# Hybrid mLSTM and delta-rule block on one core: outputs fetched back during the last group, the first z job split ahead, last quarters in token order, sigmoids by tanh

## The chip, the core and the metric

The kernel runs on one core of one Trainium2 chip. The metric is device time in microseconds (us). The kernel before takes 2027.0 us, the median of three runs (2022.27 to 2036.63). Engines are called as in the profile: PE is TensorE, PEld its weight loads, DVE is VectorE, ACT is ScalarE, POOL is GpSimd and SP is SyncE. SP issues the loads of weights, POOL and ACT issue the other transfers.

## What is computed

One layer, batch 1, 256 tokens, width 2048, in fp32. Cut to what matters here:

```python
h = rms_norm(x, norm_mix_w) * (1 + scale_m) + shift_m     # mod = silu(c) @ W_ada + b_ada gives shift, scale, gate
proj = h @ w_in
# branch A: mLSTM, 4 heads, both directions
h_a = rms_norm(mlstm_fwd(q_a, k_a, v_a, i, f) + mlstm_bwd(...))
y_a = (sigmoid(a_o) * h_a) @ w_branch_a
# branch B: gated delta rule, 16 heads, both directions
qkv = silu(depthwise_conv(b_qkv))                          # q and k are l2-normalised
log_decay = -exp(A_log) * softplus(b_a + dt_bias)
o_b = rms_norm(gdn_fwd(q_b, k_b, v_b, beta, log_decay) + gdn_bwd(...))
y_b = (o_b * silu(b_z)) @ w_branch_b
# merge, output projection, SwiGLU, final norm
x = x + gate_m * ((sigmoid(merge_a) * y_a + sigmoid(merge_b) * y_b) @ w_out)
x = x + gate_f * ((silu(hf @ w_gate) * (hf @ w_up)) @ w_down)    # hf = modulated rms_norm(x)
return rms_norm(x, norm_final_w)
```

## The kernel before

**The tiling.** Every large product is a sum of three: a weight tile `raw` of 1 MB comes by SP's queue, ACT rounds half of it to `wh` (L157, L182), DVE forms the remainder `wl = raw - wh` (L158, L183), and PE multiplies both with the high and low part of the activations. A *half* (two of the four k blocks of a `raw` tile, both tokens' tiles of 128) is 12 matmuls: four with `wh` and the high part (L200), four with `wh` and the low part (L201), four with `wl` and the high part (L203). `raw`, `wh` and `wl` have three buffers each, and the sums over the modulation weights (`ada`, L125 and L126, 1 MB each) use the same three `raw` buffers. A job (`tjob`, or `fjob` for output in transposed form) goes through eight halves and ends with a function `done` that takes the result out of PSUM. Names of tiles carry the job: z for the gate of the delta rule, v, o and a for the mLSTM's values, output gate and q/k, ma and mb for the merge gates, b for the delta rule's q, k and v, then yb, ya, o, gt, up and d.

**The order.** Jobs stand in the list `fills`, and `fill(n)` emits n of their halves between the small matmuls of the recurrences. A scheduler then sets the order of the instructions on each engine from the whole program. Only what is wrapped in `order(...)` stays in the order in which it was written. Each engine runs its own list in order, and so does each queue of DMAs: an instruction that waits holds up what stands behind it.

**The stages**, by the profiled execution: the first projections (up to 131 us), the first z job with the gates, softplus and the convolutions (131 to 180), the delta rule in four groups of four heads (180 to 985), the mLSTM with the projection y_b (985 to 1140), y_a, the output projection o (its last quarter at 1290 to 1298), gate and up, and d, whose last quarter and the final norm end the kernel.

**The first z job.** `z_job(0, 3)` makes three halves ahead (`early`), and these and all its later halves are pinned by `order`. Each later half is made only when its own step is reached. Meanwhile `gates` works out softplus by a polynomial on DVE (L377 to L395), the decay `alpha` by ACT's Exp (L397), stores it by POOL (L398) and reads it back broadcast (`al`, L279). The first reader is the scan `dec` on DVE (L544). The convolutions run on ACT and DVE (L298, L300, L301).

**The delta rule's outputs.** Each head's output `obt` is stored to DRAM by ACT (`ob_d[g]`, L773), 128 KB a head. After the fourth group, the pools of the delta rule are closed. Then `o_load` (L891 to L893) fetches each group's four heads back, 512 KB, by POOL's queue into `o4` (two buffers in the pool `ml`), and `o_split` (L897, L898) makes the high part `obh` on ACT and the low part `obl` on DVE. `obh` and `obl` are the activations of y_b, group 0 being the first four k blocks. The pool `fr` (padded rows, convolution results, q, k, v and decays of the delta rule) lives until the end of the fourth group.

**The mLSTM** loads q/k, v, the output gate (`sgo`, L906) and decays by POOL, two heads at a time. `sgo` has two buffers, so the load for heads 2 and 3 waits until heads 0 and 1 have used theirs (L971). `psc`, `pden` and `ph` are its matmuls.

**Activations.** `keep` (L308) takes the results of the v, o, ma and mb jobs through ACT (L313) and stores them. For o, ma and mb the function is Sigmoid. Silu is used by the convolutions (L301) and the z jobs (L328), Exp by the gates, Sqrt by the norms. A change of function between these sets puts an ACT_TABLE_LOAD in front of the instruction.

**Last quarters.** The jobs o and d end with a quarter that is taken token by token (`by_token`, L216 to L226): all 12 matmuls of token 0 are written before those of token 1, without `order`. When a token is done, `residual` (L1084 to L1086) and the norm follow on DVE and ACT.

## Time and profile before

| what | value |
|---|---|
| median of 3 runs | 2027.0 us |
| profiled execution, its own time | 2026.32 us |
| its span | 2024.5 us |
| PE busy | 1948.6 us (96%) |
| DVE busy | 1386.4 us (68%) |
| ACT busy | 1036.8 us (51%) |
| POOL busy | 95.2 us (5%) |
| mean granted PE clock | 0.985 |
| DMA | 485.65 MB, mean 240 GB/s |

The span is the profiled execution from its first to its last instruction, and its own time is 1.8 us longer. A busy share says how long an engine worked, not that it worked at its full clock: the granted clock is listed apart. Idle time of an engine matters only where a later end depends on it. For PE, the waits after the first 131 us, listed by what they waited for, are the shortest way in.

### The profile page before, as it was taken

The numbers are of one execution on the slowest core, as the hardware profiler recorded it, in microseconds if no ns is written. First come the engines' busy times: TensorE is split into PE (matmuls) and PEld (weight loads), VectorE is DVE, ScalarE is ACT, GpSimd is POOL, SyncE is SP. The second block draws the span as 40 slices with busy tenths as digits, with TensorE's granted clock in tenths as the row PEclk, the third lists the DMA queues.
The fourth block names the chain that finished last, engine by engine and source line by source line (L and its number), as shares of the span: only waits on it lengthen the run. The fifth ranks groups of instructions, "written<-read, shape, count | busy, mean of one in ns | idle before, by whom it ended". The sixth has DMA issues, their size and how long they took to land.

```text
span 2024.5 us, 27066 instructions
## 1 busy us (share of the span) xinstructions
PE 1948.6 (96%) x10374; PEld 1709.0 (84%) x10374; DVE 1386.4 (68%) x2059; ACT 1036.8 (51%) x1571; POOL 95.2 (5%) x181
## 2 busy tenths in 40 slices
PE   8998999999999999999799999899999999999997
PEld 6777889989889988989678888788888888888886
DVE  5777887778878778865577679766666665555554
ACT  3146748755774667555443444454444444444443
POOL 0001201100100011000200000000000000000000
PEclk9999999999999999999899999999999999999999
DMA  9986674567666665776887679556767666555653
GB/s 400 420 338 193 194 238 158 172 189 260 203 218 214 220 219 206 242 275 214 300 294 265 226 261 419 203 208 240 259 239 259 248 229 229 191 206 206 208 203 130
DMA packets 78324, 485.65 MB, mean 240 GB/s; under 512 B 10201, under 2 KB 15585, under 8 KB 23793
## 3 DMA queue, kind: packets, MB, share of 16 engines
q1 hardware_dynamic: 63360, 450.95, 61.2%
q0 software_dynamic: 7520, 17.88, 4.0%
q10 hardware_dynamic: 7314, 15.10, 2.0%
q8 instruction: 81, 1.33, 0.3%
q14 instruction: 49, 0.40, 0.1%
HBM read 467.07 MB, written 16.82 MB: 239 GB/s over the span
## 4 chain that ended last, share of the span: by engine, by line
PE 72%; DVE 11%; DMA 9%; ACT 5%; issue 3%; POOL 0%; SPq 0%; ACTq 0%; DVEq 0%; POOLq 0%
PE acc_up L201 4%; PE acc_up L203 4%; PE acc_up L200 4%; PE acc_d L200 4%; PE acc_d L201 4%; PE acc_d L203 4%; PE acc_gt L200 4%; PE acc_gt L201 4%; PE acc_gt L203 4%; DMA ra<-ada 3%; PE acc_a L161 2%; PE acc_o L203 2%; PE acc_o L200 2%; PE acc_o L201 2%; PE acc_b L161 2%
## 5 line engine op out<-in xcount | busy, mean ns | idle before, releaser
L126 DVE SCALAR_TENSOR_TENSOR ada<-ada,crow 128x2048 f32<-128x2048 f32 x64 | 146.5, 2289 | 50.6 <-DMA ada<-ada 50.6
L183 DVE TENSOR_TENSOR wl_d<-raw_d,wh_d 128x1024 fp32r<-128x1024 f32 x88 | 107.7, 1224 | 102.3 <-ACT wh_d L182 100.3
L183 DVE TENSOR_TENSOR wl_up<-raw_up,wh_up 128x1024 fp32r<-128x1024 f32 x88 | 107.6, 1225 | 99.3 <-ACT wh_up L182 99.3
L182 ACT ACTIVATE wh_d<-raw_d 128x1024 fp32r<-128x1024 f32 x88 | 92.9, 1056 | 128.5 <-PE acc_d L201 122.9
L182 ACT ACTIVATE wh_gt<-raw_gt 128x1024 fp32r<-128x1024 f32 x88 | 92.9, 1056 | 120.7 <-PE acc_gt L201 73.2
L182 ACT ACTIVATE wh_up<-raw_up 128x1024 fp32r<-128x1024 f32 x88 | 93.0, 1056 | 119.2 <-PE acc_up L201 72.5
L183 DVE TENSOR_TENSOR wl_gt<-raw_gt,wh_gt 128x1024 fp32r<-128x1024 f32 x88 | 107.0, 1224 | 67.5 <-ACT wh_gt L182 46.7
L161 PE MATMUL acc_b<-hh,wh_b 128*128 128x256 f32 x576 | 140.0, 285 | 5.5 <-ACT wh_b L157 5.5
L161 PE MATMUL acc_b<-hl,wh_b 128*128 128x256 f32 x576 | 137.6, 281 | 0.0
L200 PE MATMUL acc_gt<-wh_gt,hfh 128*128 128x512 f32 x352 | 136.0, 386 | 0.0
L201 PE MATMUL acc_gt<-wh_gt,hfl 128*128 128x512 f32 x352 | 135.2, 384 | 0.0
L200 PE MATMUL acc_up<-wh_up,hfh 128*128 128x512 f32 x352 | 133.4, 379 | 0.0
L201 PE MATMUL acc_up<-wh_up,hfl 128*128 128x512 f32 x352 | 133.4, 379 | 0.0
L200 PE MATMUL acc_d<-wh_d,ffh 128*128 128x512 f32 x344 | 130.8, 380 | 0.0
L201 PE MATMUL acc_d<-wh_d,ffl 128*128 128x512 f32 x344 | 130.8, 380 | 0.0
L511 PE MATMUL first<-x,raw 128*128 128x256 f32 x512 | 114.5, 382 | 7.1 <-ACT x L504 7.1
L161 PEld LDWEIGHTS acc_b<-hh,wh_b 128*128 128x128 f32 x576 | 111.7, 194 | 8.5 <-ACT wh_b L157 6.6
L158 DVE TENSOR_TENSOR wl_b<-raw_b,wh_b 128x1024 fp32r<-128x1024 f32 x72 | 87.3, 1219 | 45.5 <-ACT wh_b L157 45.4
L511 PEld LDWEIGHTS first<-x,raw 128*128 128x128 f32 x512 | 96.0, 190 | 25.6 <-ACT x L504 13.1
L161 PEld LDWEIGHTS acc_b<-hl,wh_b 128*128 128x128 f32 x576 | 111.7, 194 | 1.8 <-issue 1.7
L157 ACT ACTIVATE wh_b<-raw_b 128x1024 fp32r<-128x1024 f32 x72 | 75.3, 1056 | 55.8 <-DMA raw_b<-winb 29.3
L182 ACT ACTIVATE wh_o<-raw_o 128x1024 fp32r<-128x1024 f32 x64 | 67.4, 1057 | 66.1 <-PE acc_o L201 30.7
(369 smaller groups left out, 5025.7 us busy)
## 6 DMA issues: line engine op xcount, KB each, us to landing
ada<-ada SPq DMA_DIRECT2D x64, 1024.0 KB, 5.2
raw_gt<-wgu SPq DMA_DIRECT2D x44, 1024.0 KB, 5.0
raw_up<-wgu SPq DMA_DIRECT2D x44, 1024.0 KB, 5.0
raw_d<-wd SPq DMA_DIRECT2D x44, 1024.0 KB, 4.9
raw_b<-winb SPq DMA_DIRECT2D x36, 1024.0 KB, 5.2
ra<-ada SPq DMA_DIRECT2D x32, 1025.0 KB, 15.7
raw<-win SPq DMA_DIRECT2D x16, 1024.0 KB, 14.5
raw_z<-wint SPq DMA_DIRECT2D x16, 1024.0 KB, 5.7
```

The costliest lines, as they stand in the source:

```text
L126: V.scalar_tensor_tensor(raw, raw, 1.0, row_c[:, :D], ALU.mult, ALU.mult, accum_out=mod[:, c0 + b : c0 + b + 1])
L157: S.activation(wh, raw[:, k0 : k0 + 8], AF.Copy)
L158: V.tensor_tensor(wl, raw[:, k0 : k0 + 8], wh.bitcast(F32), ALU.subtract)
L161: PE.matmul(o, wh[:, k], both(x, k0 + k).rearrange("p a b -> p b a"), start=k0 + k + i == 0, stop=False)
L182: order(S.activation(wh, raws[u][:, k0 : k0 + 2], AF.Copy), early)
L183: order(V.tensor_tensor(wl, raws[u][:, k0 : k0 + 2], wh.bitcast(F32), ALU.subtract), early)
L200: order(PE.matmul(ps[t], tok(xh, kk, t), turns(wh[:, k]), start=kk == 0, stop=False), early and steps > 1)
L201: PE.matmul(ps[t], tok(xl, kk, t), turns(wh[:, k]), start=False, stop=False)
L203: PE.matmul(ps[t], tok(xh, kk, t), turns(wl[:, k]), start=False, stop=kk == last)
L511: PE.matmul(first[o], raw[:, o], x[:, b], start=b == 0 and o % 2 == 0, stop=b == KB - 1 and o % 2 == 1)
```

## The change

It has four parts.

1. A z job with `early` and one step keeps two further halves made ahead at each step, all of them pinned. Only `z_job(0, 3)` is such a job.
2. The matmuls of the last quarters (`by_token`) are pinned: all of token 0, then all of token 1.
3. `fr` gets an exit stack of its own and is closed when the fourth group (g == 3) begins. In its room a pool `op` of three buffers takes `o4` of groups 0 to 2. Their loads are issued in the fourth group, and that of group 3 goes into one buffer of `ml` after it. The three splits are made in front of the mLSTM, two halves apart. `sqh` goes from two buffers to one.
4. Sigmoid becomes tanh of half the argument. `keep` scales by 0.5, and the `+1` goes into the multiplication with the projections y_b and y_a (L1003 and L1013 of the changed kernel), the factor 0.5 into the row `gm`, through which the output projection passes anyway. The mLSTM's gate gets an instruction of its own on ACT (L980 of the changed kernel, 128x1024, one per head).

The diff, cut to its core:

```diff
             if k0:
                 pump()
                 if u == len(chunks) - 1:
                     done(ps)
+            while early and steps == 1 and len(made) < min(2, len(todo) - 1 - n):
+                made.append(halves(*todo[n + 1 + len(made)]))
             yield True
...
-                    PE.matmul(ps[t], tok(xh, kk, t), wh, start=False, stop=False)
-                    PE.matmul(ps[t], tok(xl, kk, t), wh, start=False, stop=False)
+                    order(PE.matmul(ps[t], tok(xh, kk, t), wh, start=False, stop=False))
+                    order(PE.matmul(ps[t], tok(xl, kk, t), wh, start=False, stop=False))
                 for k in range(4):
                     kk = last - 3 + k
-                    PE.matmul(ps[t], tok(xh, kk, t), turns(w[k // 2][1][:, k % 2]), start=False, stop=kk == last)
+                    order(PE.matmul(ps[t], tok(xh, kk, t), turns(w[k // 2][1][:, k % 2]), start=False, stop=kk == last))
...
-    fr = pool(sx, "fr", side="right")
+    sf, so = ExitStack(), ExitStack()
+    fr = pool(sf, "fr", side="right")
...
     def keep(dst, fn, name):
+        scale = 0.5 if fn == AF.Tanh else 1.0
...
-                S.activation(ev[:, t], ps[t], fn)
+                S.activation(ev[:, t], ps[t], fn, scale=scale)
...
-            keep((v_d, o_d)[i][h], (AF.Copy, AF.Sigmoid)[i], f"{'vo'[i]}{h}"),
+            keep((v_d, o_d)[i][h], (AF.Copy, AF.Tanh)[i], f"{'vo'[i]}{h}"),
...
-            keep((ma_d, mb_d)[i][g], AF.Sigmoid, f"m{'ab'[i]}{g}"),
+            keep((ma_d, mb_d)[i][g], AF.Tanh, f"m{'ab'[i]}{g}"),
...
+    def o_load(g, where, bufs):
+        o4 = where.tile([P, 4, T], F32, tag="o4", bufs=bufs, name=f"o4_{g}")
+        G.dma_start(o4, ob_d[g].rearrange("h p t -> p h t"))
+        return o4
+
+    o4s = []
     invert(0)
     for g in range(4):
+        if g == 3:
+            sf.close()
+            op = pool(so, "op", side="right")
...
             pieces = stream(4 * g + 2 * p + 4)
+            if g == 3:
+                o4s += [o_load(i, op, 3) for i in ((0, 1), (2,))[p]]
...
-        sq = ml.tile([P, DV_A], F32, tag="sqh", bufs=2, name=f"sqh{h}")
+        sq = ml.tile([P, DV_A], F32, tag="sqh", bufs=1, name=f"sqh{h}")
...
         V.reciprocal(ss, ss)
+        S.activation(so, so, AF.Copy, scale=0.5, bias=0.5)
...
-                V.tensor_tensor(mg[:, t, g * 512 : (g + 1) * 512], gt[:, t], ps[t], ALU.mult)
+                V.scalar_tensor_tensor(mg[:, t, g * 512 : (g + 1) * 512], gt[:, t], 1.0, ps[t], ALU.add, ALU.mult)
...
-                V.tensor_tensor(gt[:, t], gt[:, t], ps[t], ALU.mult)
+                V.scalar_tensor_tensor(gt[:, t], gt[:, t], 1.0, ps[t], ALU.add, ALU.mult)
...
     cores = steps(mlstm(0), mlstm(1))
-    o4s = [o_load(g) for g in range(2)]
     every[0] = 0
-    fill(2)
+    o4s.append(o_load(3, ml, 1))
     next(cores)
-    fill(6)
-    for g in range(2):
+    for g in range(3):
+        fill(2)
         o_split(g, o4s[g])
-        o4s.append(o_load(g + 2))
-        fill(1)
+    fill(4)
     next(cores)
-    fill(5)
-    o_split(2, o4s[2])
     fill(1000)
+    so.close()
...
-                V.tensor_scalar(dg[:, e], ident, mod[:, c : c + 1], None, ALU.mult)
+                V.tensor_scalar(dg[:, e], ident, mod[:, c : c + 1], factor, ALU.mult, ALU.mult)
...
-    row(2, gm, wp)
+    row(2, gm, wp, 0.5)
```

**Where instructions move.** First DVE, in the first z job. `u`, `s` and `poly` are steps of the softplus polynomial, `cv` the convolutions, and `wl_z_2_0` the remainder that z's fifth half (third tile, first half) needs. Before:

```order
L386 SCALAR_TENSOR_TENSOR poly<-poly,s_801 128x256 x2
L300 SCALAR_TENSOR_TENSOR cv_2_1070<-pad_136,pk,cv_2_1070 128x256
L386 SCALAR_TENSOR_TENSOR poly<-poly,s_801 128x256
L300 SCALAR_TENSOR_TENSOR cv_2_1070<-pad_136,pk,cv_2_1070 128x256
L300 SCALAR_TENSOR_TENSOR cv_0_1339<-pad_138,pk,cv_0_1339 128x256
L386 SCALAR_TENSOR_TENSOR poly<-poly,s_801 128x256
L183 TENSOR_TENSOR wl_z_2_0_812<-raw_z_2_809,wh_z_2_0_811 128x1024
L183 TENSOR_TENSOR wl_z_2_2_828<-raw_z_2_809,wh_z_2_2_827 128x1024
L183 TENSOR_TENSOR wl_z_3_0_854<-raw_z_3_851,wh_z_3_0_853 128x1024
```

In the changed kernel:

```order
L381 TENSOR_TENSOR u<-u,gden 128x256
L183 TENSOR_TENSOR wl_z_2_0_784<-raw_z_2_781,wh_z_2_0_783 128x1024
L183 TENSOR_TENSOR wl_z_2_2_808<-raw_z_2_781,wh_z_2_2_807 128x1024
L303 SCALAR_TENSOR_TENSOR cv_0_987<-pad_140,pk,cv_0_987 128x256
L303 SCALAR_TENSOR_TENSOR cv_1_1020<-pad_134,pk,cv_1_1020 128x256
L386 TENSOR_TENSOR s_811<-u 128x256
L303 SCALAR_TENSOR_TENSOR cv_1_1020<-pad_134,pk,cv_1_1020 128x256
L388 TENSOR_SCALAR poly<-s_811 128x256
```

`wl_z_2_0` now stands right behind `u`; before, 13 polynomial and convolution steps stood between them. The same steps now come behind it, and further on five remainders of the next job (v) stand among the steps from `poly` to `sp`, from which the decay is made. On the same engine the first scan `dec` (L544 before, L548 now) stands behind the remainder of v's eighth half. Before, it stood behind that of v's second half.

Second, POOL and ACT around the outputs of the delta rule. POOL before, from the last of the delta rule's own transfers:

```order
L607 DMA uu_6547<-inst_d_121 16x1024
L625 DMA inv_d_125<-uu_6547 64x16x32 x2
L652 DMA cg_7828<-inv_d_125 32x512 x4
L893 DMA o_0_8861<-ob_d_114 128x4x256
L893 DMA o_1_8863<-ob_d_115 128x4x256
L902 DMA mkq_8927<-kq_d_94 128x4x256
L904 DMA vt_8929<-v_d_98 128x1024
L906 DMA sgo_8931<-o_d_102 128x1024
```

and now:

```order
L611 DMA uu_6547<-inst_d_121 16x1024
L861 DMA o_0_8110<-ob_d_114 128x4x256
L861 DMA o_1_8112<-ob_d_115 128x4x256
L861 DMA o_2_8476<-ob_d_116 128x4x256
L629 DMA inv_d_125<-uu_6547 64x16x32 x2
L656 DMA cg_7832<-inv_d_125 32x512 x4
L861 DMA o_3_8870<-ob_d_117 128x4x256
L912 DMA mkq_8872<-kq_d_94 128x4x256
L914 DMA vt_8874<-v_d_98 128x1024
```

The loads of groups 0 to 2 stand ahead of the fourth group's own `inv_d` and `cg` transfers. That of group 3 has the place that group 0's had. ACT now, from the last store of the delta rule on:

```order
L777 DMA ob_d_117<-obt_8854 128x256
L182 ACTIVATE wh_yb_0_2_9290<-raw_yb_0_9272 128x1024
L907 ACTIVATE obh<-o_0_8110 128x1024
L907 ACTIVATE obh<-o_1_8112 128x1024
L907 ACTIVATE obh<-o_2_8476 128x1024
L182 ACTIVATE wh_yb_1_0_9343<-raw_yb_1_9341 128x1024
L317 ACT_TABLE_LOAD
L317 ACTIVATE ev_ma_9248<-acc_ma_0_9082 128x512
L317 ACTIVATE ev_ma_9248<-acc_ma_1_9083 128x512
L182 ACTIVATE wh_yb_1_2_9359<-raw_yb_1_9341 128x1024
```

Before, `wh_yb_1_0`, the table load and both `ev_ma` stood ahead of the first `obh`. The gate's new instruction for head 2 stands between the last `wh_yb` of y_b's second job and the first of its third, that for head 3 two halves further. DVE's remainders `obl` of groups 0 to 2 likewise stand ahead of `wl_yb_1_0`.

Third, PE at the end of the output projection (`acc_o_0` is token 0). Before:

```order
L224 MATMUL acc_o_0_11286<-wl_o_3_0_11401,mgh 128x512 x2
L220 MATMUL acc_o_1_11287<-wh_o_3_2_11404,mgh 128x512
L221 MATMUL acc_o_1_11287<-wh_o_3_2_11404,mgl 128x512
L224 MATMUL acc_o_1_11287<-wl_o_3_0_11401,mgh 128x512
L224 MATMUL acc_o_0_11286<-wl_o_3_2_11405,mgh 128x512 x2
```

Now:

```order
L223 MATMUL acc_o_0_11294<-wh_o_3_2_11412,mgl 128x512
L226 MATMUL acc_o_0_11294<-wl_o_3_0_11409,mgh 128x512 x2
L226 MATMUL acc_o_0_11294<-wl_o_3_2_11413,mgh 128x512 x2
L222 MATMUL acc_o_1_11295<-wh_o_3_0_11408,mgh 128x512
L223 MATMUL acc_o_1_11295<-wh_o_3_0_11408,mgl 128x512
```

Token 0's last matmul was the 21st of the quarter's 24 and is now the 12th. In the job d it was the 16th and is now the 12th. On ACT the number of table loads goes from 57 to 45. Ten of those that go stood in front of Sigmoid or of the Silu or Exp that followed one, in the stage of the delta rule; two stood in the first z job, where `sz` (Silu) now comes ahead of the Exp.

More of the change, by code (lines that the diff above doesn't have):

```diff
@@ L889, in hybrid_block @@
     obh, obl = big(bigC, F32R, "obh"), big(bigC, F32R, "obl")
-    def o_load(g):
-        o4 = ml.tile([P, 4, T], F32, tag="o4", bufs=2, name=f"o4_{g}")
-        G.dma_start(o4, ob_d[g].rearrange("h p t -> p h t"))
-        return o4
     def o_split(g, o4):
@@ L1065, in hybrid_block, with row @@
     S.dma_start(x1, xr)
-    def row(part, dst, rp):
+    def row(part, dst, rp, factor=1.0):
         for g in range(4):
```

## The prediction

> **What bounds the kernel now.** I read the shares of busy time first, then what PE waits for after the first stage, then the timeline of each engine around the longest waits. The waits of PE from 131 us on (what waited, for what; us in total, times, longest):
>
> ```profile
> PE acc_yb L200 <- ACT obh L897: 12.6, 1, 12.6
> PE pxn L1171 <- ACT xn L1164: 8.9, 7, 5.3
> PE acc_z L203 <- DVE wl_z L183: 7.2, 1, 7.2
> PE acc_b L161 <- ACT wh_b L157: 5.5, 6, 1.6
> PE vps L555 <- ACT vf L301: 3.3, 2, 3.1
> ```
>
> PE is busy for 96% of the span, so it sets the time nearly everywhere, and only work taken off it or its own waits are worth anything. No matmul is removed here. What can be won is in these rows and in the clock behind each wait. The change aims at four of the five; `acc_b` waits for weights and keeps its 5.5 us.
>
> **The first z job.** The rows are start, duration, instruction, and in brackets the idle time before it with its releaser:
>
> ```profile
> 151.12 0.42 DVE L377 TENSOR_TENSOR u<-u,gden 128x256 f32<-128x256 f32 x1
> ...
> 156.23 3.49 DVE L183 TENSOR_TENSOR wl_z<-raw_z,wh_z 128x1024 fp32r<-128x1024 f32 x3
> ```
> ```profile
> 157.50 2.08 PE L203 MATMUL acc_z<-wl_z,hh 128*128 128x512 f32 x4 [7.17 <-DVE wl_z L183]
> ...
> 172.62 0.38 PE L200 MATMUL acc_v<-wh_v,hh 128*128 128x512 f32 x1
> ...
> 1057.75 0.38 PE L200 MATMUL acc_yb<-wh_yb,obh 128*128 128x512 f32 x1
> ...
> 1060.34 0.38 PE L200 MATMUL acc_yb<-wh_yb,obh 128*128 128x512 f32 x1
> ```
>
> PE stops at 157.50 - 7.17 = 150.33. The remainder it needs comes after the softplus steps. The new order puts it right behind `u`, so it is there at about 151.5 + 1.2 = 152.7, and the wait is 2.4 us. From that point to the end of v's first half (172.62) stand 4 + 12 + 12 + 12 + 12 = 52 matmuls. The two rows of y_b are the starts of neighbouring halves: 12 matmuls in 2.59 us, 0.216 each, so 52 take 11.2 us where nothing holds PE. The new end is 152.7 + 11.2 + 0.2 (z's seventh half waits briefly for its remainder behind the same softplus steps, with v's first eight matmuls in front as cover) = 164.1: 8.5 us earlier.
>
> Two things take some back. First the clock (the last two figures but one are the granted clock and the DMA share):
>
> ```profile
> 150.00:160.00 10.00, 2.83 (x8) 2.05 (x7) 9.25 (x19) 4.63 (x11) 0.00 (x0) 0.75 0.09 12
> ...
> 378.50:384.00 5.50, 5.50 (x35) 5.50 (x35) 4.59 (x8) 3.04 (x6) 0.00 (x0) 0.69 0.23 52
> ```
>
> The second row follows a wait of PE of 1.9 us: 0.31 of 5.5 us is lost, 1.7 us. A wait of 2.4 us will mostly cost the same; I take 1.3. Second, the decay:
>
> ```profile
> 164.86 0.42 ACT L397 ACTIVATE s<-sp 32x256 f32<-32x256 f32 x1 [0.77 <-DVE sp L395]
> ...
> 173.42 0.69 DVE L544 TENSOR_TENSOR_SCAN dec<-al,cst 128x256 f32<-128x256 f32 x1 [0.24 <-DMA al<-alpha_d]
> ```
>
> From the Exp to the first scan it takes 8.6 us, through two DMAs of POOL. Five remainders of v now stand ahead of `sp`, and each waits until PE gives a buffer back. So the Exp comes at about 173 instead of 165, and the scan at 181.5. It stands ahead of the remainder of v's ninth half on DVE. Four scans and that remainder end near 184.6, and PE asks for it at 164.1 + 7 x 2.59 + 1.7 = 183.9. I charge 1. The term is -8.5 + 1.3 + 1.0 = **-6.2**, from -8.5 to -3 (the decay 3 us later than reckoned).
>
> **The table loads.** Twelve of 1.28 us go. Most lie beside PE's own work and are worth nothing while `wh` stays ahead. The exception:
>
> ```profile
> 595.35 1.28 ACT L313 ACT_TABLE_LOAD   x1
> ...
> 597.75 1.28 ACT L301 ACT_TABLE_LOAD   x1
> ...
> 599.04 0.42 ACT L301 ACTIVATE vf<-cv 128x256 f32<-128x256 f32 x1
> ```
> ```profile
> 594.33 1.51 DVE L300 SCALAR_TENSOR_TENSOR cv<-pad,pk,cv 128x256 f32<-128x256 f32 x3
> ```
> ```profile
> 599.51 0.69 PE L555 MATMUL vps<-cst,vf 128*128 128x128 f32 x2 [3.08 <-ACT vf L301]
> ```
> ```profile
> 599.00:608.00 9.00, 8.49 (x45) 8.02 (x46) 3.26 (x13) 6.40 (x19) 0.00 (x0) 0.63 0.54 202
> ```
>
> `cv` is ready at 595.84, so without the two loads `vf` starts 2.57 earlier and PE's wait shrinks from 3.1 to 0.5. Behind it the clock stands at 0.63: of 8.49 us busy, 3.1 are lost to it. A wait of 0.5 should leave it alone. The term is -2.6 - 2.9 = **-5.5**, from -2.6 (clock unchanged) to -6. The Trainium skill ("TensorE: Matmul & The Clock Gate", Part 1, the HAM clock gate) says that the clock falls after a whole idle window of about 3.4 us; the rows after waits of 3.1 and 1.9 us contradict it, and by the rule the term would be -2.6. The Trainium skill ("ScalarE: Activation LUTs", What ACT_TABLE_LOAD costs) puts 2.66 us on a switch, with a drain behind the load; here the next instruction starts 1.29 us after the load began, and at the page's price the term would be -8.3.
>
> **The outputs fetched back.**
>
> ```profile
> 804.94 0.33 ACTq L773 DMA_DIRECT2D ob_d<-obt  x1
> ...
> 980.33 0.33 ACTq L773 DMA_DIRECT2D ob_d<-obt  x1
> ...
> 996.59 1.06 ACT L897 ACTIVATE obh<-o 128x1024 fp32r<-128x1024 f32 x1 [8.61 <-DMA o<-ob_d]
> ```
> ```profile
> 830.49 0.86 POOL L625 DMA_DIRECT2D inv_d<-uu  x1 [21.31 <-DVE uu L639]
> ...
> 985.70 1.57 POOL L893 DMA_DIRECT2D o<-ob_d  x2 [125.88 <-ACT wh_yb L182]
> ```
> ```profile
> 997.70 1.22 PE L200 MATMUL acc_yb<-wh_yb,obh 128*128 128x512 f32 x2 [12.59 <-ACT obh L897]
> ```
> ```profile
> 985.00:1000.00 15.00, 2.37 (x6) 1.36 (x6) 3.55 (x3) 5.07 (x6) 6.29 (x10) 0.60 0.96 351
> ...
> 997.70:1001.60 3.90, 3.86 (x8) 2.65 (x9) 3.90 (x4) 1.06 (x1) 1.35 (x3) 0.51 1.02 387
> ```
> ```profile
> raw_yb<-wbb SPq DMA_DIRECT2D x3, 1024.0 KB, 8.3
> o<-ob_d POOLq DMA_DIRECT2D x4, 512.0 KB, 11.7
> ob_d<-obt ACTq DMA_DIRECT2D x1, 128.0 KB, 4.4
> ```
>
> PE ends at 997.70 - 12.59 = 985.11. POOL names ACT as the releaser, but that instruction is one of several it waits for; the store of 980.33 lands 4.4 us later, just before. Then the load takes 10.9 us in a stretch in which the DMA share is 0.96. Now the loads of groups 0 to 2 stand on POOL between 808 and 830, where it is idle for 21.31 us: three issues of 0.8 us. The last of the stores that they read is that of 804.94; with the 4.4 us it has landed at 809.4, and `inv_d` at 830.49 behind them isn't late. `obh` must still wait for the last stores, since it takes their room: it starts at about 985.7 and ends 1.06 later. PE goes on at 986.8 instead of 997.7: -10.9. The clock may come back too: behind the wait, 3.9 us ran at 0.51, so 0 to 1.9; I take 1.0.
>
> Against it: group 3's `o4` lands as `o4` of group 0 did (996.6), and PE asks for it at 986.8 + 6 x 2.59 = 1002.3, in time. The weights of y_b's fourth tile are issued when the fourth half's remainder is made, near 991; with 8.3 to 11.7 us they land at 999 to 1003, so PE waits 0 to 3, and DVE has `obl` of group 3, one `ada` sum and the scans `mdec` there: together 0 to 5, I take 1.5.
>
> The gate's new instruction is what ACT can be held by:
>
> ```profile
> 1043.92 1.42 DVE L971 SCALAR_TENSOR_TENSOR hs<-hs,ssh,sgo 128x512 f32<-128x512 f32 x2
> ```
> ```profile
> 1045.63 0.53 POOL L906 DMA_DIRECT2D sgo<-o_d  x1 [2.42 <-DVE hs L971]
> ...
> 1050.78 0.53 POOL L906 DMA_DIRECT2D sgo<-o_d  x1 [4.62 <-DVE hs L971]
> ```
> ```profile
> DMA to landing us min/median/max: 4.5/8.4/13.8
> ```
>
> In the old clock, `sgo` of head 2 will be issued near 1047.4 (ACT takes both heads' squares first) and land 8.4 later, at 1055.8. Correction and `wh` of y_b's third job, 1.06 each, end at 1057.9, and PE asks at 1057.75. So 0.2; with 13.8 us it is 5.6, with 4.5 nothing. I take 0.5. The term is -10.9 - 1.0 + 1.5 + 0.5 = **-9.9**, from -13 to -3.
>
> **The last quarters.**
>
> ```profile
> 1297.18 0.69 DVE L1084 TENSOR_TENSOR tmss<-acc_o,gm 128x512 f32<-128x512 f32 x1 [3.08 <-PE acc_o L224]
> ...
> 1299.98 0.67 DVE L1084 TENSOR_TENSOR tmss<-acc_o,gm 128x512 f32<-128x512 f32 x1
> ```
> ```profile
> 2011.34 0.69 DVE L1084 TENSOR_TENSOR tmss<-acc_d,gf 128x512 f32<-128x512 f32 x1 [4.59 <-PE acc_d L224]
> ...
> 2015.33 0.68 DVE L1084 TENSOR_TENSOR tmss<-acc_d,gf 128x512 f32<-128x512 f32 x1
> ```
>
> Token 1's chain stands behind token 0's on DVE (2.8 and 4.0 us later), and PE has both ready by then. Token 0 ends 9 matmuls earlier in o and 4 in d: 9 x 0.216 = **-1.9** and 4 x 0.216 = **-0.9**. Both chains move with it. The steps between stay as they are, so half of each is the lower bound. The multiplications with `+1` replace products on DVE, which has slack there: 0.
>
> **Sum.** -6.2 - 5.5 - 9.9 - 1.9 - 0.9 = -24.4, from 2026.3 to 2001.9 for a profiled execution. The median of the runs lies 0.7 above the profiled one, so 2002.6.
>
> **Rivals.** *The wait comes back inside y_b.* DMA is full there (0.96), and behind every load stands another: the fourth weight tile, group 3's `o4` or `sgo` holds PE for 7 us instead of 2. For it speaks the share; against it that 1 MB of `o4` leaves the stretch. Then the term is about -3: 2009.5. *The decay gives the z job's gain back.* DVE is busy for 9.25 of 10 us there, and all of group 0 hangs on the scan. If the chain, not PE, sets the end of group 0's first phase, the -6.2 go: 2008.8. Against it: the scan and the remainders behind it came out only 1 us late above. *Slower: the loads block POOL's queue.* `inv_d` and the blocks of the fourth group stand behind three loads that also wait for the room of `fr`. If one buffer of it were read until the group's end (the store of 980.33), `inv_d` would come 150 us later. Every microsecond past 830.5 delays the group's blocks, and from about 875 on the change is slower than before by more than it can win: 2047 or more. Against it: the tiles in that room belong to the first phase, whose results this very queue carries out before the loads. *A wait of 3 us doesn't lower the clock*: then the clock's 2.9 us stay where they are, 2005.5; the rows speak against it.
>
> **How the numbers follow.** Forecast 0.64, wait inside y_b 0.17, decay 0.12, clock 0.03, POOL 0.04. A difference under 1% (20.3 us, so 2006.7) is about what a measurement can't tell from none. The forecast lies below it nine times in ten, the three smaller gains one time in four: faster 0.67, within 1% 0.29, slower 0.04. The lower end has all terms at their best, -8.5 - 6 - 13 - 2.8 = -30, with a few us for the runs' spread: 1994. The upper has two of the smaller-gain cases at once: 2016.
>
> **What would show it.** In the new profile PE's wait for `wl_z` is 2 to 3 us; `vps` waits for `vf` 0.5; `o<-ob_d` is issued three times between 797 and 815 and `obh` starts near 985.7 less the shift of about 12; PE's wait there is under 3; `pxn` 5.3 becomes 3.4. I am wrong if DVE waits for `al` by several us ahead of `wl_v`, if `acc_yb` or ACT's `sgo` has waits above 3 us, or if POOL's `inv_d` waits for an `o4`.

## The result

The changed kernel takes 2009.05 us (median of four runs, 2002.91 to 2012.95) against 2025.65 us for the kernel before on the same chip (2022.27 to 2036.63): a ratio of 0.9914, 95% interval 0.9894 to 0.9934. Measured again on another chip, it was 2006.64 us and 0.9905 (0.9879 to 0.9931). The ratio comes from the single runs and can differ from the quotient of the medians by up to 0.0015. The forecast was 2002.6: the sign is right, but a third of the gain is missing. The profiled execution is the slowest of the four (2012.95 us, span 2011.2), so its shifts are a little smaller than those of the medians.

What PE waits for from 131 us on, in the profile after:

```profile
PE acc_b L161 <- ACT wh_b L157: 8.8, 7, 2.5
PE pxn L1179 <- ACT xn L1172: 7.0, 7, 3.4
PE p L691 <- DVE R L663: 3.0, 1, 3.0
PE pden L956 <- DVE mdec L941: 2.6, 1, 2.6
PE acc_v L203 <- DVE wl_v L183: 2.5, 1, 2.5
...
PE acc_z L203 <- DVE wl_z L183: 2.4, 1, 2.4
```

The four waits that the change aimed at are smaller or gone: `obh` 12.6 to 0, `wl_z` 7.2 to 2.4, `xn` from a longest of 5.3 to 3.4, `vf` 3.3 to 0.7. Two new waits stand in their place: `pden`, in the stage of y_b, and `wl_v`, behind the first z job. With the clock behind them they are where most of the rest of the gain went, as the experiments show. `acc_b`, which was to keep its 5.5 us, waits 8.8 (7.9 in the second profile of the changed kernel); no run here isolates that.

I compare the kernels by shifts: the start of an instruction less its start in the kernel before, and what the shift gains or loses between two such places. The places (times of the kernel before): 218 us, the end of group 0's first phase; 586 to 609 around `vf`; 979, the last `px` of the delta rule; 1151, the first `pxm` behind y_b and the first y_a job; 1310, behind the job o.

```
              to 218   218-586  586-609  609-979  979-1151  1151-1310  1310-end
after          -2.2      +2.3     -4.8     -0.6      -4.7       -2.1      -1.4
```

The +2.3 is a wait of `p` (3.0 us, 1.7 before) with 6.8 us of half clock at 491; the second profile of the changed kernel has -1.2 there.

**The first z job.** DVE, POOL and SP in the profile after, around the decay:

```profile
151.53 2.35 DVE L183 TENSOR_TENSOR wl_z<-raw_z,wh_z 128x1024 fp32r<-128x1024 f32 x2
...
171.37 0.34 DVE L399 TENSOR_SCALAR sp<-sp,ea 128x256 f32<-128x256 f32 x1
...
185.30 0.69 DVE L548 TENSOR_TENSOR_SCAN dec<-al,cst 128x256 f32<-128x256 f32 x1 [5.23 <-DMA al<-alpha_d]
```
```profile
173.42 0.65 POOL L402 DMA_DIRECT2D alpha_d<-s  x1 [170.36 <-ACT s L401]
178.71 1.48 POOL L282 DMA_DIRECT2D al<-alpha_d  x2 [4.64 <-DMA alpha_d<-s]
```
```profile
172.87 7.10 SPq L179 DMA_DIRECT2D raw_v<-wint  x2
```

The remainder comes when it was forecast. PE starts v's second half at 165.82, 6.8 us earlier than before, and v's first result is stored 7.8 us earlier. But the scan starts at 185.30, not at 181.5: between the issue of `alpha_d` and that of `al` POOL waits 4.64 us (1.50 before), and `al` needs 6.6 more. The remainder of v that stands behind the scans is late with it, and PE waits 2.5 us and then loses half of 3.4 us to the clock. At 218 us, 2.2 of the 7.8 are left.

**The table loads.** PE's wait for `vf`, and the stretch behind it:

```profile
597.75 0.44 PE L559 MATMUL vps<-cst,vf 128*128 128x128 f32 x2 [0.73 <-ACT vf L304]
```
```profile
597.00:606.00 9.00, 8.27 (x57) 7.07 (x57) 6.07 (x21) 7.13 (x20) 0.00 (x0) 1.00 0.84 296
```

The wait is 0.73 us and the clock stays at 1.00, where it stood at 0.63.

**The outputs.** POOL's loads, ACT's split, and the places where the stage waits now (rows of POOL, ACT, DVE and PE):

```profile
805.95 2.26 POOL L861 DMA_DIRECT2D o<-ob_d  x3 [0.19 <-DMA ob_d<-obt]
825.92 0.85 POOL L629 DMA_DIRECT2D inv_d<-uu  x1 [17.72 <-DVE uu L643]
...
989.92 0.53 POOL L916 DMA_DIRECT2D sgo<-o_d  x1 [5.52 <-DMA o<-ob_d]
991.18 0.54 POOL L919 DMA_DIRECT2D bc<-mal_d  x1 [0.73 <-DMA mkq<-kq_d]
994.92 0.54 POOL L919 DMA_DIRECT2D bc<-mal_d  x1 [3.19 <-DMA vt<-v_d]
```
```profile
978.77 2.95 ACT L907 ACTIVATE obh<-o 128x1024 fp32r<-128x1024 f32 x3 [1.23 <-DMA ob_d<-obt]
...
1006.97 1.06 ACT L980 ACTIVATE sgo<-sgo 128x1024 f32<-128x1024 f32 x1 [6.78 <-DMA sgo<-o_d]
```
```profile
1007.85 0.69 DVE L923 TENSOR_TENSOR_SCAN mdec<-bc,cst 128x256 f32<-128x256 f32 x1 [4.77 <-DMA bc<-mal_d]
```
```profile
979.88 0.70 PE L200 MATMUL acc_yb<-wh_yb,obh 128*128 128x512 f32 x2
...
1010.40 0.80 PE L956 MATMUL pden<-ones,mdec 128*128 128x1 f32 x3 [2.59 <-DVE mdec L941]
```
```profile
992.00:998.00 6.00, 6.00 (x29) 5.12 (x28) 3.69 (x4) 0.76 (x1) 0.54 (x1) 1.00 1.02 396
...
1010.00:1016.00 6.00, 5.60 (x15) 3.53 (x15) 5.97 (x12) 0.69 (x1) 1.06 (x2) 0.50 0.72 242
```

The outputs are there, POOL's queue isn't blocked, and PE begins y_b without a wait, 17.8 us earlier than before. Then most of that goes again. POOL can't issue the second head's two `bc` loads until earlier transfers have landed; they are issued at 991.18 and 994.92 and land at 1007.8 and 1008.9, with DMA at 1.0 all the while. DVE waits 4.77 us for the first, PE 2.59 for DVE, and behind that wait the clock is at 0.5 for 10.2 us.

### The profile page after: what moved, and what is told of

Its sections match the earlier page's. It is cut to its first block, busy times and chain, and to the rows that moved or that the text cites. A ratio compares the mean times of both kernels' runs of the same rounds, so it can differ in the third digit from the quotient of the medians.

```text
span 2011.2 us, 27050 instructions
## 1 busy us (share of the span) xinstructions
PE 1949.6 (97%) x10374; PEld 1707.9 (85%) x10374; DVE 1388.6 (69%) x2059; ACT 1024.7 (51%) x1563; POOL 94.7 (5%) x181
## 4 chain that ended last, share of the span: by engine, by line
PE 76%; DMA 9%; DVE 7%; ACT 5%; issue 2%; POOL 0%; ACTq 0%; SPq 0%; DVEq 0%; POOLq 0%
PE acc_up L201 4%; PE acc_up L203 4%; PE acc_up L200 4%; PE acc_d L201 4%; PE acc_d L200 4%; PE acc_d L203 4%; PE acc_gt L200 4%; PE acc_gt L201 4%; PE acc_gt L203 4%; DMA ra<-ada 3%; PE acc_b L161 3%; PE acc_o L203 2%; PE acc_o L201 2%; PE acc_o L200 2%; PE acc_a L161 2%
```

## The experiments

**Each kernel's gain by place.** All numbers are us; the ratio is to the kernel before on the same chip.

```
              median   ratio [95%]               to 218  586-609  979-1151  1151-1310
after         2009.05  0.9914 [0.9894, 0.9934]     -2.2     -4.8      -4.7       -2.1
after_again   2006.64  0.9905 [0.9879, 0.9931]     -8.8     -5.7      -1.3       -2.1
no_ahead      2011.70  0.9948 [0.9931, 0.9964]     -0.1     -5.7      -5.2       -1.9
sigmoid       2006.44  0.9926 [0.9901, 0.9951]     +0.6     +0.2      -8.9       -2.1
no_o          2011.50  0.9945 [0.9930, 0.9960]     -8.2     -5.7      -1.8       -2.1
no_token      2012.83  0.9937 [0.9914, 0.9960]     -2.0     -5.7      -2.2        0.0
pin_v         2004.30  0.9905 [0.9885, 0.9926]     -2.4     -5.7      -4.3       -2.1
bc_first      2004.97  0.9898 [0.9865, 0.9932]     +0.5     -5.7      -5.0       -1.9
store_fix     2002.63  0.9905 [0.9870, 0.9940]     -0.4     -5.7      -4.8       -2.1
z_sooner      2007.74  0.9921 [0.9892, 0.9949]     -0.7     -5.7      -7.1       -2.1
sgo_late      1996.25  0.9864 [0.9839, 0.9890]     -2.3     -6.2     -14.9       -2.1
combo         1996.88  0.9871 [0.9846, 0.9896]     -1.0     -5.7     -16.5       -2.1
exp_warm      1993.67  0.9841 [0.9817, 0.9864]     -7.6     -5.7     -16.1       -2.1
```

Single times of one kernel lie 2 to 16 us apart, so a term of 2 to 6 us can be read from the places and hardly from the medians.

**Undoing one part each.** *no_ahead* takes the two halves split ahead out again:

```
-            while early and steps == 1 and len(made) < min(2, len(todo) - 1 - n):
-                made.append(halves(*todo[n + 1 + len(made)]))
```

> The changed kernel without the two halves of the first z job split ahead; all else as changed. Theory (the decay gives most of the gain back): the first z job was worth 2.2 us at the end of group 0's first phase, so the median is about 2011 (2 above the changed kernel's 2009.05). In the profile the wait for wl_z is back at 7 us, v's first half ends near 172.6, and the first scan of dec starts near 173.5 again, with no wait of DVE for al above 1 us. Rival (the decay's lateness is only hidden cover, and the 8.5 us are worth their full 6.2 later): about 2015.3.

Measured 2011.70 us. PE's wait for `wl_z` is 7.2 again, the store of `alpha_d` goes out at 165.69 and the scan starts at 173.78 with a wait of 0.48. The shift at 218 is -0.1: the part was worth 2.1 us there in the first profile of the changed kernel, as the theory said, and 8.7 in the second, where the store went out sooner (below). The medians lie 2.7 us apart and the ratios 0.0034, about 7 us, which would be the rival's; with these spreads they don't decide.

*sigmoid* sets the gates by Sigmoid again:

```
-            keep((v_d, o_d)[i][h], (AF.Copy, AF.Tanh)[i], f"{'vo'[i]}{h}"),
+            keep((v_d, o_d)[i][h], (AF.Copy, AF.Sigmoid)[i], f"{'vo'[i]}{h}"),
...
-        S.activation(so, so, AF.Copy, scale=0.5, bias=0.5)
...
-                V.scalar_tensor_tensor(mg[:, t, g * 512 : (g + 1) * 512], gt[:, t], 1.0, ps[t], ALU.add, ALU.mult)
+                V.tensor_tensor(mg[:, t, g * 512 : (g + 1) * 512], gt[:, t], ps[t], ALU.mult)
...
```

> The changed kernel with the gates taken out of ACT by Sigmoid again instead of by tanh, so the table loads come back; all else as changed. Theory: the table loads were worth what the trace lost at vf, 4.5 us (wait 2.4, clock 2.2): median about 2013.5, vps waits about 3 us for vf and the clock behind it is near 0.63. In the y_b stage ACT has no correction of sgo, so its two waits of 5.6 and 6.8 us for sgo go; if these hold PE there (the rival), 3 to 5 us come back and the median is 2009 or less.

The place is as the theory has it, the whole is not. The wait came back:

```profile
PE vps L559 <- ACT vf L304: 3.1, 1, 3.1
```

and between 586 and 609 this kernel alone gains nothing, where eleven others gain 5.7 to 6.2 and the first profile of the changed kernel 4.8. Yet its median, 2006.44, is no higher, and its ratio, 0.9926, is higher by less than the intervals tell. In its profile y_b's stage has 3.4 us of half clock instead of 10.2, though `pden` waited 3.6 us without any correction on ACT. What it gained elsewhere is within what such stretches differ by from run to run; the medians don't show the 5.7 us, and I leave their worth in the whole at what the place shows.

*no_o* loads all four groups' outputs behind the delta rule again:

```
-            if g == 3:
-                o4s += [o_load(i, op, 3) for i in ((0, 1), (2,))[p]]
...
-    o4s.append(o_load(3, ml, 1))
+    o4s = [o_load(g, ml, 2) for g in range(2)]
...
```

> The changed kernel with the loads of all four groups' o4 back behind the delta rule's last group, in the room and order of before; gates by tanh and the rest as changed. Theory: the net worth of the early loads is 5.8 us, since 11 of the 17.8 us that PE gains at the first matmul of y_b are spent again up to 1063 on waits for sgo, bc and on the clock behind pden; the median is about 2015, the wait for obh about 12 us, and the waits for pden and sgo are shorter than 2 us. Rival (those waits come from the gate's new instruction alone and not from the loads): they stay at 5 to 7 us here too, and the median is 2019 or more.

Measured 2011.50, below what either said; the ratio, 0.9945 for 0.9914, would be a loss of about 6 us and so near the theory's.

```profile
PE acc_yb L200 <- ACT obh L905: 12.0, 1, 12.0
PE acc_yb L200 <- ACT wh_yb L182: 1.1, 1, 1.1
```

The wait for `obh` is back, `pden` has none, and from 979 to 1151 this kernel gains 1.8 us on the one before. The nine profiles with the early loads and the old order of `sgo` gain 1.3 to 8.9, 4.8 on the mean. So at this place 12 us of wait were taken away and about 3 were won.

*no_token* leaves the last quarters to the scheduler (no `order` around the three matmuls of L222 to L226).

> The changed kernel with the last quarters of o and d left to the scheduler's order (the two tokens' matmuls interleaved as before). Theory: 2.1 us come back at o and 0.9 at d, 3.0 together: median about 2012, pxn waits 5.3 us again. Rival (both chains end with token 1's, which does not move): 0 to 1.5, median 2009 to 2010.5.

`pxn` waits 5.3 us again, and from 1151 to 1310 nothing is gained where all others gain 1.9 to 2.1. From 1798 to the end it gains 0.5, the changed kernel 1.3. The theory holds: 2.1 and about 0.9.

**Why `al` is late.** *after_again* is the changed kernel, unchanged.

> The changed kernel once more, beside the three that follow. Theory (the times of the changed kernel fall in two groups, by whether the clock is halved behind the 2.4 us wait for wl_z, and so whether al comes in time): single times of about 2003 and of 2008 to 2013, median about 2009; in the profile either a half clock of 3.4 us at 153 with a wait of DVE for al of about 5 us, or neither. Rival (the spread is chance all over the program): no such pair.

Its profile has neither the half clock at 153 nor the wait for `al`:

```profile
172.41 0.64 POOL L402 DMA_DIRECT2D alpha_d<-s  x1 [169.35 <-ACT s L401]
174.56 1.48 POOL L282 DMA_DIRECT2D al<-alpha_d  x2 [1.51 <-DMA alpha_d<-s]
```
```profile
172.81 0.33 SPq L179 DMA_DIRECT2D raw_v<-wint  x1
```
```profile
180.04 0.69 DVE L548 TENSOR_TENSOR_SCAN dec<-al,cst 128x256 f32<-128x256 f32 x1
```

The shift at 218 is -8.8. The pair is there, but the two groups of times are not: this execution took 2007.88 us, for it lost elsewhere (4.9 us at `pden`). One late store isn't what the runs spread by.

*pin_v* orders the last softplus steps and the Exp ahead of v's first job:

```
...
-            order(S.activation(wh, raws[u][:, k0 : k0 + 2], AF.Copy), early)
+            order(S.activation(wh, raws[u][:, k0 : k0 + 2], AF.Copy), early or pin)
...
+            keep((v_d, o_d)[i][h], (AF.Copy, AF.Tanh)[i], f"{'vo'[i]}{h}"), pin=i == 0 and h == 0,
...
-        S.activation(s2[32:64], sp[32:64], AF.Exp)
+        order(S.activation(s2[32:64], sp[32:64], AF.Exp))
```

> The changed kernel with the last softplus steps and the Exp, in the order that is recorded, ahead of the remainders of v's first job; all else as changed. Theory (the z job's gain is lost because alpha_d and al are late behind v's remainders): the store of alpha_d is issued 5 to 7 us earlier, near 167, the scans start before 180 without a wait of DVE for al above 1 us, and PE has no wait for wl_v above 1 us between 185 and 195; the shift against the kernel before is about -6 at 218 us instead of -2.15; median about 2005. Rival (v's remainders behind the softplus steps hold PE instead): a wait for wl_v of 2 us or more at 160 to 170, the shift at 218 stays at -2 to -3, median 2008 to 2010.

The store goes out at 169.54 and the scan starts at 178.95, after a wait of 2.33. Still the shift at 218 is -2.4. PE's waits from 150 to 200 us:

```profile
PE acc_z L203 <- DVE wl_z L183: 2.4, 1, 2.4
PE acc_v L200 <- ACT wh_v L182: 2.0, 1, 2.0
PE acc_v L203 <- DVE wl_v L183: 1.3, 1, 1.3
```

The rival's place is right: v's halves hold PE. DVE has no time to give away there; what the decay wins, the remainders lose. The median, 2004.30, is the theory's, but by the place it can't have come from here.

*z_sooner* takes the 2.4 us wait itself away, by recording z's second half one step sooner:

```
-            fill(2 if i in (4, 6, 8, 10) else 1)
+            fill(2 if i in (1, 6, 8, 10) else 1)
```

> The changed kernel with the z job's second half recorded one softplus step sooner, so that the remainder PE waits for at 150 us stands on DVE right behind the reciprocal and ahead of the product u; one more remainder of v then stands ahead of sp. Theory (the 2.4 us wait halves the clock in 6 of 8 profiles, that delays the Exp by 1 us and the landing of al by 5): the wait for wl_z is 0.3 to 0.9 us, no half clock between 150 and 158, the shift at 218 us against the kernel before is -6 to -9 in place of -2, single times no longer reach 2012; median 2003 to 2005. Rival (the Exp is late because DVE has no time for it there, clock or not): al still lands at 184 or later, DVE waits for it 3 us or more, the shift at 218 is -1 to -4, median 2008 to 2010.

The wait for `wl_z` is 0.4 and the clock isn't halved there, but `al` is as late as before, and PE waits at `ptr`:

```profile
173.79 0.64 POOL L402 DMA_DIRECT2D alpha_d<-s  x1 [170.74 <-ACT s L401]
178.41 1.48 POOL L282 DMA_DIRECT2D al<-alpha_d  x2 [3.97 <-DMA alpha_d<-s]
```
```profile
PE ptr L438 <- DVE tr L427: 5.4, 1, 5.4
PE acc_z L203 <- DVE wl_z L183: 0.4, 1, 0.4
```

So the clock is not the cause, and my theory fell in that form. What all thirteen profiles have in common is the order of two issues:

```
             store of alpha_d   behind raw_v of 1 MB by   al issued after   scan after
before            165.58              6.92                    2.15             7.84
no_ahead          165.69              6.92                    2.15             8.08
pin_v             169.54              8.70                    2.15             9.41
after_again       172.41              3.55                    2.15             7.63
no_o              172.48              3.56                    3.31             8.47
store_fix         173.26              0.54                    5.45            12.15
sgo_late          173.26              0.54                    5.32            11.87
bc_first          173.29              0.55                    5.37            12.17
sigmoid           173.38              0.55                    5.45            12.29
after             173.42              0.55                    5.28            11.88
no_token          173.72              0.55                    5.24            11.71
z_sooner          173.79              1.69                    4.61            11.64
combo             173.85              1.69                    5.25            12.12
```

In the kernels that split ahead, a `raw_v` load of 1 MB goes out at 171.2 to 173.2. A store issued before it takes 2.2 to 3.3 us to the issue of `al`; one issued up to 1.7 us behind it takes 4.6 to 5.5. In each of the eight kernels where it is behind, the store lands 0.2 to 0.7 us after that load. In the changed kernel the half clock only shifted the Exp by 1 us (172.70 for 171.68), enough to turn the order round.

**Where the y_b stage loses it.** *bc_first* issues `bc` ahead of the head's other loads:

```
+        bc = ml.tile([P, 2, T], F32, tag="bc", bufs=2, name=f"bc{h}")
+        for d in range(2):
+            G.dma_start(bc[:, d], mal_d[d, h].partition_broadcast(P))
         kq = ml.tile([P, 4, T], F32, tag="mkq", bufs=2, name=f"mkq{h}")
...
```

> The changed kernel with the mlstm's bc loads issued ahead of kq, vt and sgo of the same head. Theory (the y_b stage loses 2.6 us at pden plus 10.2 us of half clock to bc, which comes last of each head's loads): DVE's wait of 4.8 us for bc and PE's wait for pden are gone or under 0.5, the half clock at 1010 too; the stage from the last px of the delta rule to the first pxa, 78.1 us now, takes 71 to 74; median 2003 to 2005. Rival (mkq or the scans ahead of the remainder of y_b's fourth half take its place): a wait of 1.5 us or more for psc or wl_yb, the stage 76 to 79, median 2007 to 2011.

```profile
PE acc_yb L200 <- ACT wh_yb L182: 2.9, 1, 2.9
PE psc L932 <- DMA mkq<-kq_d: 2.5, 1, 2.5
```
```profile
987.12 0.76 POOL L915 DMA_DIRECT2D mkq<-kq_d  x1 [5.60 <-DMA o<-ob_d]
```

`pden` has no wait left, but two others do, the half clock of 10.2 us too, and the stage to the first `pxa` takes 81.1 us. The rival holds: the wait only moved, and what POOL now holds back is the second head's `mkq`. The median, 2004.97, is the theory's, but single times go from 1994.82 to 2010.51.

*store_fix* takes the correction of the o gate off ACT's queue in this stage:

```
...
                 S.activation(ev[:, t], ps[t], fn, scale=scale)
+            if whole:
+                S.activation(ev, ev, AF.Copy, scale=0.5, bias=0.5)
...
+            keep((v_d, o_d)[i][h], (AF.Copy, AF.Tanh)[i], f"{'vo'[i]}{h}", i == 1),
...
-        S.activation(so, so, AF.Copy, scale=0.5, bias=0.5)
```

> The changed kernel with the o gate's 0.5 t + 0.5 applied by ACT where the o job's result is taken out, not in the y_b stage; the table loads stay away. Theory (the waits of ACT for sgo hardly hold PE, since with the sigmoids back pden still waited 3.6 us): the waits of ACT for sgo are gone, the stage from the last px to the first pxa takes 77 to 79 us, median 2008 to 2010. Rival (ACT's waits for sgo of 5.6 and 6.8 us are what costs the stage its gain): the stage takes 74 or less and the median is 2005 or less.

ACT's two waits for `sgo` are gone, `pden` waits 3.8 us, the stage takes 81.3 us (a little more than the theory's 77 to 79): the gate's instruction isn't the cost. The median, 2002.63, is the rival's, but the interval of the ratio holds the changed kernel's.

*sgo_late* issues the `sgo` loads one step later, when `den` is made:

```
-        so = ml.tile([P, 2, DV_A], F32, tag="so", bufs=2, name=f"sgo{h}")
-        G.dma_start(so, o_d[h])
...
         ss = ml.tile([P, 2], F32, tag="ssh", bufs=2, name=f"ssh{h}")
         yield
+        so = ml.tile([P, 2, DV_A], F32, tag="so", bufs=2, name=f"sgo{h}")
+        G.dma_start(so, o_d[h])
```

> The changed kernel with the mlstm's sgo loads issued after the step that makes den, not with the head's other loads. Theory (from the end of the delta rule to pden the transfers, with a DMA share of 1.0 for 30 us, set the end; whatever is last waits): 1 MB less ahead of bc lets it land 2.5 us or more earlier; pden waits under 1.5 us instead of 2.6 to 4.9, the stage from the last px to the first pxa takes 73 to 76 us instead of 78 to 81; median 2003 to 2006. Rival (the order and the issue by POOL, not the bytes, set when bc lands): pden or psc waits 2.5 us or more as before, stage 78 to 81, median 2006 to 2010.

Measured 1996.25 us, ratio 0.9864 (0.9839 to 0.9890), below the theory's 2003. All of PE's waits of the stage, POOL's two `bc` loads of the second head, the first of its scans, and the transfers:

```profile
PE acc_yb L200 <- ACT obh L907: 0.7, 1, 0.7
PE acc_yb L201 <- DVE obl L908: 0.6, 1, 0.6
PE psc L930 <- DMA mkq<-kq_d: 0.2, 1, 0.2
```
```profile
979.31 0.54 POOL L917 DMA_DIRECT2D bc<-mal_d  x1
985.26 0.54 POOL L917 DMA_DIRECT2D bc<-mal_d  x1 [5.42 <-DMA o<-ob_d]
```
```profile
998.14 0.69 DVE L921 TENSOR_TENSOR_SCAN mdec<-bc,cst 128x256 f32<-128x256 f32 x1 [1.87 <-DMA bc<-mal_d]
```
```profile
990.00:996.00 6.00, 5.84 (x30) 4.84 (x28) 4.71 (x10) 2.00 (x2) 2.35 (x4) 1.00 1.01 378
996.00:1002.00 6.00, 6.00 (x34) 5.38 (x34) 4.13 (x11) 0.17 (x1) 1.28 (x2) 1.00 1.01 410
```

DMA is as full as before. The same bytes move, but those that PE needs first come first: `pden` has no wait, there is no half clock up to the first `pxa`, and 979 to 1151 gains 14.9 us instead of 4.7. (The stage to the first `pxa` takes 62.6 us here, but that matmul also stands earlier among y_b's, so I read the gain at 1151.)

The run doesn't tell the bytes ahead of `bc` from its place in POOL's list. In all fourteen profiles POOL has at most eight of its transfers under way, and in this stage the ninth waits for an earlier one to land: in the profile after, `sgo` of 989.92 waits for `o` of 979.42, and the two `bc` behind it for the `mkq` and `vt` of the first head. (Each waits on the semaphore, the counter of landings, that the transfer eight places before it raises, so this limit is written in the program.) With `sgo` taken out, the second head's two `bc` are the eighth and ninth transfer and no longer the tenth and eleventh. Counted from the load of group 3's `o4`, they are issued 7.3 and 5.1 us sooner and land 5.1 us sooner; from issue to landing they take no less (18.8 and 14.0 us, 16.7 and 14.0 in the changed kernel). In *bc_first* the ninth transfer was the `mkq` for which PE then waited.

*combo* has both edits, *z_sooner* and *sgo_late*, and `vt` behind `bc`.

> Both edits above, and vt behind bc of the same head. Theory: the two gains add, stage 72 to 75, shift at 218 -6 to -9, median 1997 to 2002. Rival (the transfers only move their wait): stage 78 or more, median 2003 or more.

Measured 1996.88: the stage's gain is there (71.3 us, 16.5 up to 1151), the z job's is not, since its store is again behind `raw_v`.

*exp_warm* is *sgo_late* with the Exp's table loaded sooner:

```
             V.scalar_tensor_tensor(poly, poly, 2.0 / c, s2, ALU.add, ALU.mult)
+            if c == 3:
+                S.activation(w0.tile([P, 1], F32, name="warm"), poly[:, 0:1], AF.Exp)
```

> The kernel with the late sgo loads, and besides one activation of a single column by Exp some 5 us ahead of the softplus's Exp, so that the table load stands there and not between wh_v and the Exp; its result is used by nothing. Theory (alpha_d's store is late by whom it is issued behind: 0.5 to 1.7 us after a 1 MB load of raw_v it takes 4.6 to 5.5 us until al can be issued, ahead of that load 2.2 to 3.3): the Exp starts at 171.8 or sooner, the store is issued before the raw_v load of 172.7 to 172.9, the first scan comes at 179.5 to 181.5 with a wait for al under 1.5 us, whether or not the clock is halved at 153; wl_v's wait of 2.5 us near 188 is gone, the shift at 218 us is -5 to -9 in place of -2.3, median 1990 to 1994. Rival (the landing is late because the transfers of that time are many, whichever is issued first): the scan stays at 184 or later, the shift at -1 to -3.5, median 1995 to 1999.

```profile
172.58 0.65 POOL L404 DMA_DIRECT2D alpha_d<-s  x1 [169.51 <-ACT s L403]
174.76 1.48 POOL L282 DMA_DIRECT2D al<-alpha_d  x2 [1.54 <-DMA alpha_d<-s]
```
```profile
172.99 0.33 SPq L179 DMA_DIRECT2D raw_v<-wint  x1
```
```profile
180.25 0.69 DVE L550 TENSOR_TENSOR_SCAN dec<-al,cst 128x256 f32<-128x256 f32 x1
```
```profile
152.40:155.90 3.50, 3.17 (x8) 2.54 (x9) 3.50 (x9) 1.84 (x5) 0.00 (x0) 0.51 0.33 51
```

The clock is halved behind the 2.4 us wait here too, and all the same the store is 0.41 us ahead of the load, the scan starts at 180.25 without a wait, `wl_v` holds nobody, and the shift at 218 is -7.6. This is shown, then: the store 0.7 us sooner is worth 5.3 us at 218. The median is 1993.67 us (five runs, 1989.90 to 1998.24), the ratio 0.9841 (0.9817 to 0.9864): better than the kernel before and the changed kernel, while its interval still touches that of *sgo_late*.

## Why the prediction was right and wrong

The measured gain of 0.9% lies in the case "within 1%", to which the prediction gave 0.29. (Its weights add up to 0.66 for faster and 0.30 for that case, not 0.67 and 0.29.)

- **The bound** was read rightly: PE's waits and the clock behind them are the time. After 131 us the waits of 0.3 us and more add up to 51.5 us before and 38.5 after: these 13.0 are nearly the whole 13.3 between the two profiles. One row moved that the prediction left alone: `acc_b`, 3.3 us more. The clock gave nothing where 2.6 were reckoned (2.9 and 1.0 gained, 1.3 lost): PE worked 36.9 us at half clock before and 40.1 after. In the second profile of the changed kernel it was 26.3 at the same sum of waits (38.8): half of the difference, 6.9 us, is what that would save, and the span is 5.3 us shorter. Much of the spread of the times seems to lie there: of the changed kernel's four runs the slowest had a mean granted clock of 0.988 and the fastest 0.992.
- **The first z job**, -6.2 forecast, -2.2 in the first profile, -8.8 in the second. The wait for `wl_z` (2.4) and v's second half (7.2 earlier forecast, with the clock's 1.3; 6.8 measured) were right. The step that failed is "From the Exp to the first scan it takes 8.6 us": it is 12.6 (172.70 to 185.30). I had taken the row from a stretch in which the last 1 MB load had gone out 6.9 us earlier and moved it to where one goes out 0.55 us ahead of the store. The 1.0 that I charged for the decay became about 5. The rival "the decay gives the z job's gain back" named the place but gave it too little chance; the test that I set ("DVE waits for `al` by several us ahead of `wl_v`") found it.
- **The table loads**, -5.5 forecast: -4.8, and -5.7 in nearly all later profiles. Wait (0.73 for 0.5) and clock (1.00) came as reckoned. The -8.3 that the prediction works out beside it could not have come: PE's whole wait for `vf` was 3.1 us, so with the clock's 2.9 no more than 6.0 was to be had.
- **The outputs**, -9.9 forecast, -4.7. The wait went (12.6 to 0), `obh` started at 978.77, `inv_d` wasn't late, and the wait for the fourth tile's `wh_yb` cost 1.1. The step that failed is "together 0 to 5, I take 1.5": I listed the scans `mdec` among DVE's work and never asked when `bc`, the last of a head's loads on POOL, would land. With it, "The clock may come back too ... I take 1.0" turned into a loss of 4.9 (PE worked 9.7 of the 10.2 us at half clock). ACT waited 5.6 and 6.8 us for `sgo`, a sign of being wrong that the prediction names, but the 0.5 for it can't be told from nothing: in *store_fix*, without these waits, the stage took no less. The rival "the wait comes back inside y_b" is what happened, at `pden` and not at the weights, `o4` or `sgo` that I named, and *sgo_late* shows that 14.9 us were to be had at this place.
- **The quarters**, -1.9 and -0.9: -2.1 and about -0.9. Right by their mechanism, since *no_token* loses just these.
- **POOL's queue blocked**: no; `inv_d` came at 825.92. **A wait of 3 us doesn't lower the clock**: no, as the last section counts.

The terms that went by a place's own rows came out within 1 us. Both that failed hang on a transfer: one I moved into another traffic with its old time, the other I left out.

## What to carry to other kernels

When a wait is removed, look up which transfer PE will ask for next, in the order of need, and compare that with the order in which the loads are issued: with DMA at 1.0, and with a limit on how many transfers a queue has under way, a load that is needed 25 us later (here `sgo`, first used by DVE at 1035) must not stand ahead of one that is needed now (`bc`, for `pden` at 1010). A duration from issue to landing belongs to its traffic; when a step moves, ask which large load goes out just ahead of it. A term of 2 to 6 us in a kernel whose runs spread by 10 is read from the shift at its own place.

## What the runs showed of the hardware

- **A small store waits for the large load issued ahead of it.** `alpha_d` has 32 KB and goes out by POOL, `raw_v` 1 MB by SP. Issued 0.54 to 0.55 us behind it, `al` follows 5.24 to 5.45 us after the store (4.61 and 5.25 at 1.69 us); issued ahead of it or 3.5 us behind the one before, 2.15 to 3.31. The Trainium skill ("DMA: Bandwidth & Descriptors", Queues, rings and completion order) says that each DMA engine takes turns between the queues packet by packet. By that the store should hardly have noticed the load, and none of the eight profiles with the store right behind it agrees.
- **Waits of 2 us lower the clock often, not always.** In all fourteen profiles after 131 us, a half clock began between a wait's start and 4 us after its end in 1 of 90 PE's waits of 1 to 1.5 us, 23 of 66 of 1.5 to 2, 18 of 26 of 2 to 2.5, 24 of 25 of 2.5 to 3.5, and 14 of 14 longer ones. The same wait of 2.4 us at 150 us was followed by it in 8 of 10 profiles. The Trainium skill ("TensorE: Matmul & The Clock Gate", Part 1) asks for a whole idle window of about 3.4 us; the stretches do last 3.41 us or a multiple of it, as its window has it (but for the last, which the program's end cuts off), but here a wait of two thirds of a window was mostly enough.
